# The latent keys' norm factor through DRAM, and the first heads' queries ahead of the first keys, in a two-layer decoder trunk

## The chip, the core and the metric

The kernel runs on one core of a Trainium2 chip. Five engines work side by side, each through its own instructions in order: PE (TensorE, matrix products into the PSUM memory), DVE (VectorE), ACT (ScalarE), POOL (GpSimd) and SP (SyncE, which here issues nearly all DMA transfers). They wait for one another by semaphores. The metric is the device time of one execution in microseconds (us). Before the change it is 1119.46 us, the median of three runs (1118.91 to 1119.87).

## The reference

The input is x of 512 tokens by 1024 features in float32. Two layers follow, each a token mixer and a squared-ReLU MLP (1024 to 4096 to 1024) with norms ahead and residuals. The first layer's mixer is a "forgetting" attention of 16 heads. The second is a multi-head latent attention of 8 heads, whose keys and values come from one compressed stream. The part that the change touches is the projection ahead of that second attention:

```python
src = rms_norm(stream, kv_norm_g)
kv_a = src @ w_kv_a                                   # 256 latent + 64 rotary columns
c_kv = rms_norm(kv_a[..., :KV_LORA_RANK], kv_a_norm_g)
k_rope = apply_rope(kv_a[..., KV_LORA_RANK:], cos, sin)
kv_b = (c_kv @ w_kv_b)                                # k_nope (128 a head) and v (128 a head)
c_q = rms_norm(h @ w_q_a, q_a_norm_g)                 # 384 latent columns
q = c_q @ w_q_b                                       # 128 without and 64 with rotation, a head
s = q_nope . k_nope + q_rope . k_rope                 # then scale, causal softmax, times v
```

A norm's factor 1/sqrt(mean of squares + eps) is one number per token. For `c_kv` it must be applied to tiles that have the features along the 128 partitions and the 512 tokens along the free axis, so each partition needs the whole row of 512 factors.

## The kernel before

**Arithmetic.** PE multiplies in a rounded float32 (fp32r). Each operand is split into a high part (a cast on ACT) and a low part (a subtraction on DVE), and a product is three matmuls: high by high, high by low, low by high (`three`, lines 272 to 281). `split` (204) makes the two parts of an activation tile: one ACT instruction, then one DVE instruction that waits for it. Almost everything is a 128 x 512 tile.

**Weights.** All weights lie in DRAM in the order in which they are used, cut into pieces (`pieces`, 75; the host's `_pack`, 1455, lays them out alike). Two raw buffers receive them by DMA from SP (`fetch`, 217), ACT casts the high part (`cast_piece`, 222) and DVE subtracts the low part (`low_piece`, 235). In the stage of the change this is done by hand with `prepare(n)` (1179): cast piece n, make its low part, and fetch piece n + 2 into the raw buffer that this frees. KA is the first of six pieces "ka" (the two compressing products). Behind them, KA+6 is "qb_r" (the rotary queries' weights of the first two heads, 384 columns), KA+7 "kvb_n" (the keys' weights of four heads, 1024), KA+8 "qb_n" (the first two heads' other queries, 768), KA+9 "kvb_v" (values, 1024).

**The stage.** From line 1177 to 1310 the order of the instructions on PE, DVE and ACT is as written (`order["on"]` chains each engine's instructions); SP's and POOL's is not, a planner places those. The planner also places everything behind line 1310 (the attention), and may put it ahead of the written chain's later instructions on the same engine. The stage computes `kv[0]`, `kv[1]` (latent keys), `krp` (rotary key) and `ql[0..2]` (latent queries) in PSUM, each in two halves (`low_rank`). Two factors along the tokens are made in it:

- The stream's norm factor (1203 to 1212): `token_sums` on PE puts the sums of squares of 128 tokens into each of four columns, `rsqrt_of(alone=True)` makes 1/sqrt on DVE with eleven tiny instructions, and then two DMAs turn the result: a write of 2 KB to DRAM (`line`) and a read of that row to all partitions (`row`, tile tag `rstd`). The row comes back with token p + 128 b at place 4 p + b, and is read with a stride of four elements (1227).
- The latent keys' norm factor (1252 to 1266): sums and 1/sqrt as before, and then `along_tokens(rs_kv)` (345): on PE, four products with the identity, two instructions each, put the row into a PSUM bank (`krow`, bank tag `tp`), and ACT copies it to SBUF (`kr`).

With `kr`, DVE scales both latent tiles by gain and factor (`ts`, 1270), ACT casts their high parts, DVE makes the low ones (`ckv`). Between these stand the third latent query (`low_rank(ql[2])`, `high(2)`, `low(2)`), the split of the rotary key (`krh`, `krl`), a square and two additions for the queries' factor. Then PE's order is: rotary queries `qb_r` (9 matmuls), keys of heads 0 to 3 from `ckv` (6 matmuls each, 1289), the queries' token sums, queries of heads 0 and 1 (9 matmuls each, 1302), and four blocks of values (`v_gen(0)`, 6 each). Three PSUM banks "acc" go round among these; a product waits until the tile three before it on "acc" has been split. `shift` and `rotate` turn the rotary queries, `stacked(a)` splits them, and POOL does most of the queries' 1/sqrt (`rs_q`). Then the attention begins, with further projections as filler between its steps.

Of the kernel before, what the change touches and what calls it, by code (L numbers as in the profile page):

```python
# [74 lines left out]
def pieces():  # L75

    out = [("f", 128)]
    out += [("qk", 1024)] * 2 + [("v", 1024)] * 4
    for p in range(1, FH // 2):
        out += [("v4", 1024)] * (2 * V4_BEFORE.count(p)) + [("qk", 1024)] * 2  # L80
    out += [("fo", 1024)] * 8
    out += [("ffn0", 1024)] * 40
    out += [("ka", 1024)] * 6
    q = [("qb_r", 384), ("qb_n", 768)]
    out += [q[0], ("kvb_n", 1024), q[1], ("kvb_v", 1024)] + q + [("kvb_n", 1024)] + q + q + [("kvb_v", 1024)]
    out += [("mo", 1024)] * 8
    out += [("ffn1", 1024)] * 32
    return out
# [11 lines left out]
def trunk(ctx: ExitStack, tc: tile.TileContext, xT, wts, gains, fing, rope, out):  # L100
# [63 lines left out]
    def nm(s):  # L164
        uid[0] += 1
        return f"{s}{uid[0]}"
# [7 lines left out]
    def tt(shape=(P, S)):  # L174
        return tp_.tile(list(shape), F32, tag="t", name=nm("t"))

    def f32(ap):
        return ap.bitcast(F32)
# [147 lines left out]
    def rsqrt_of(v, mult=1.0, alone=False, tags=("rs1", "rs2")):  # L326
        y, a = (small.tile([P, v.shape[-1]], F32, tag=t, name=nm("rs"), bufs=2 if t[:2] == "rs" else 1) for t in tags)

        nc.vector.tensor_single_scalar(a.bitcast(I32), v.bitcast(I32), 1, op=ALU.arith_shift_right)
        nc.vector.tensor_scalar(y.bitcast(I32), a.bitcast(I32), -1, RSQRT_BITS, op0=ALU.mult, op1=ALU.add)  # L330
        for step in range(3):
            m = mult if step == 2 else 1.0
            if alone:
                nc.vector.tensor_tensor(a, y, y, op=ALU.mult)
                nc.vector.scalar_tensor_tensor(out=a, in0=a, scalar=-0.5 * m, in1=v, op0=ALU.mult, op1=ALU.mult)
                nc.vector.scalar_tensor_tensor(out=y, in0=a, scalar=1.5 * m, in1=y, op0=ALU.add, op1=ALU.mult)
            else:

                nc.gpsimd.tensor_tensor(a, y, y, op=ALU.mult)
                nc.gpsimd.tensor_tensor(a, a, v, op=ALU.mult)  # L340
                nc.gpsimd.tensor_scalar(a, a, -0.5 * m, 1.5 * m, op0=ALU.mult, op1=ALU.add)
                nc.gpsimd.tensor_tensor(y, a, y, op=ALU.mult)
        return y
# [716 lines left out]
    def rt2():  # L1060
        return rp2.tile([P, S], F32R, tag="r2", name=nm("r2"))

    ctxs = []
    with ExitStack() as mx:
# [139 lines left out]

        em = small.tile([P, NB], F32, tag="em", name=nm("em"), bufs=1)
        nc.vector.tensor_scalar(em, vx, EPS, 0.0, op0=ALU.mult, op1=ALU.add)
        rs = rsqrt_of(vx, alone=True)
        line = keep.tile([S], F32, name=nm("line"))

        nc.sync.dma_start(line.rearrange("(p b) -> p b", b=NB), rs)  # L1210
        row = small.tile([P, S], F32, tag="rstd", name=nm("rstd"), bufs=2)
        nc.sync.dma_start(row, line.partition_broadcast(P))
        prepare(KA + 3)
        low_rank(kv[1], w[1][:4], hk, 0)
        low_rank(ql[0], w[1][4:], hm, 0)
# [7 lines left out]
        w = [blocks(piece("ka")) for _ in range(3)]  # L1223
        rotary_low(w[0][:4], 1)
        u, o = tt(), tt()
        ub, kb = (t.rearrange("p (b q) -> p b q", b=NB) for t in (u, krp))
        nc.vector.tensor_tensor(ub, kb, row.rearrange("p (q b) -> p b q", b=NB), op=ALU.mult)
        low_rank(kv[0], w[0][4:], hk, 1)
        for e in range(2):
            nc.scalar.copy(o[e * ROPE : (e + 1) * ROPE], u[(1 - e) * ROPE : (2 - e) * ROPE])  # L1230
# [22 lines left out]
        q_acc = tt()  # L1253
        square(q_acc, ql[0])
        high(0)
        rs_kv = rsqrt_of(mean(ss, KVR, em), alone=True)
        prepare(KA + 7)
        low(0)
        low_rank(ql[1], w[2][:4], hm, 1)
        krow = along_tokens(rs_kv)  # L1260
        sqs.append(tt())
        square(sqs[0], ql[1])
        high(1)
        low(1)
        kr = tt()
        nc.scalar.copy(kr, krow)
        ts = [tt(), tt()]
        ckv = [(rt2(), rt2()) for _ in range(2)]
        for b in range(2):
            nc.vector.scalar_tensor_tensor(out=ts[b], in0=kv[b], scalar=g("kva", b), in1=kr, op0=ALU.mult, op1=ALU.mult)  # L1270
            nc.scalar.copy(ckv[b][0], ts[b])
        low_rank(ql[2], w[2][4:], hm, 1)
        high(2)
        nc.vector.tensor_tensor(ckv[0][1], ts[0], f32(ckv[0][0]), op=ALU.subtract)
        low(2)
        nc.vector.tensor_tensor(ckv[1][1], ts[1], f32(ckv[1][0]), op=ALU.subtract)
        krh, krl = split(a)
        sqs.append(tt())
        square(sqs[1], ql[2])
# [4 lines left out]

        qp = bank("sc")
        linear(qp, piece("qb_r"), cq, nk=3)
        wk = piece("kvb_n")
        a, o = tt(), tt()
        for hd in range(4):
            kp_ = bank("acc" if hd < 3 else "tp")  # L1290
            linear(kp_, wk, ckv, nk=2, at=hd * 2 * P)
# [6 lines left out]

        rs_q = rsqrt_of(mean(ss, QR, em), -float((NOPE + ROPE) ** -0.5), tags=("rq1", "rq2"))
        prepare(KA + 10)  # L1300
        qw = piece("qb_n")
        for e in range(2):
            qp = bank("acc")
            linear(qp, qw, cq, nk=3, at=e * 3 * P)
            if e == 0:
                qr[0] = stacked(a)
            qn[e] = split(qp)
        for _ in v_gen(0):
            pass
        order["on"] = ()  # L1310
# [144 lines left out]
def _pack(i):  # L1455
# [38 lines left out]
    for p in range(4):  # L1494
        qs.append(_blk(qb[:, 2 * p : 2 * p + 2, NOPE:].reshape(QR, 2 * ROPE), slice(None)))
        qs.append(np.concatenate([_blk(qb[:, 2 * p + e, :NOPE], slice(None)) for e in range(2)], axis=1))
    parts += [qs[0], ns[0], qs[1], vs[0]] + qs[2:4] + [ns[1]] + qs[4:] + [vs[1]]
    parts += [_cols(i["mla_w_out"][0], f * P, P) for f in range(8)]
    parts += up(1)
    assert [x.size // P for x in parts] == [w for _, w in PIECES]  # L1500
# [48 lines left out]
```

## Time and profile before

| | |
|---|---|
| median of three runs | 1119.46 us |
| the profiled execution: time / span | 1119.58 us / 1117.5 us |
| PE busy | 1101.2 us, 99% of the span |
| DVE, ACT busy | 781.8 us (70%), 584.0 us (52%) |
| granted PE clock | 0.998 of full speed |
| the written stage | 594 to 648 us of the span |
| the second attention | 648 to about 752 us |

The span runs from the first to the last instruction; the time has some 2.1 us more around it. In rows of the timeline, the columns are start in us, duration in us, engine, line, operation, output <- inputs, shapes, count, and in brackets the idle time of the engine before it with what ended it. Rows show line 114 for almost all instructions, because a helper there records them; tiles tell them apart. Matmuls overlap: a row's duration is the modelled time through the array (0.39 us), while their starts lie closer together. So time that PE lost is read from starts.

### The profile page before, as it was taken

Reading aid. Unit: us, or ns where it says so; the run is one execution under the profiler, and the core shown is the slowest. Engines: PE = TensorE matmul, PEld = TensorE weight load, DVE = VectorE, ACT = ScalarE, POOL = GpSimd, SP = SyncE. Lnnn points to the kernel's source line nnn. Section 1 sums busy time; section 2 is a strip of 40 time slices with the busy share of each in tenths; the row PEclk is TensorE's granted clock in tenths of the full one; section 3 lists DMA queues with packets and bytes.
Section 4 is the critical chain, followed back from the end, with each engine's and each line's share of the span. In section 5 each row is a group of like instructions: output and inputs, shape, how many; then the busy total and the mean of one; then the engine's idle time right before and its main releaser. Section 6 shows DMA issues by size and latency. Waiting matters only on the chain.

```text
span 1117.5 us, 14137 instructions
## 1 busy us (share of the span) xinstructions
PE 1101.2 (99%) x5292; PEld 911.3 (82%) x5292; DVE 781.8 (70%) x1414; ACT 584.0 (52%) x1071; POOL 13.6 (1%) x46
## 2 busy tenths in 40 slices
PE   8999999999999999999999999999999999999997
PEld 6877887888888888888888888888888888888885
DVE  6899788864566667577896889736365775765784
ACT  5566565654555454434444768624675445444622
POOL 1000000001000000000000000000000000000000
PEclk9999999999999999999999999999999999999999
DMA  5322222142724315321345212214531611611401
GB/s 191 133 93 79 77 76 94 58 151 95 276 101 143 120 38 166 101 70 29 126 132 152 73 60 76 97 55 132 174 147 57 190 55 57 207 57 38 132 1 75
DMA packets 37108, 116.90 MB, mean 105 GB/s; under 512 B 4384, under 2 KB 5024, under 8 KB 37040
## 3 DMA queue, kind: packets, MB, share of 16 engines
q1 hardware_dynamic: 36176, 114.41, 31.2%
q10 hardware_dynamic: 864, 1.60, 0.4%
q8 instruction: 41, 0.67, 0.2%
q14 instruction: 27, 0.22, 0.1%
HBM read 109.67 MB, written 6.33 MB: 104 GB/s over the span
## 4 chain that ended last, share of the span: by engine, by line
PE 93%; DVE 4%; ACT 2%; DMA 0%; issue 0%; SPq 0%; ACTq 0%
PE up L114 35%; PE go L114 19%; PE acc L114 18%; PE tp L114 8%; PE keep L114 6%; PE sc L114 6%; DVE r L114 1%; DVE t L114 1%; ACT t L114 1%; ACT r L114 1%; DMA t<-xT 0%; DVE wlo L114 0%; DVE ptl L114 0%; DVE rs L114 0%; ACT whi L114 0%
## 5 line engine op out<-in xcount | busy, mean ns | idle before, releaser
L114 PE MATMUL up<-r,r 128*128 128x512 f32 x808 | 192.6, 390 | 0.0
L114 PE MATMUL acc<-r,whi 128*128 128x512 f32 x574 | 185.7, 404 | 5.0 <-ACT whi L114 5.0
L114 PEld LDWEIGHTS up<-r,r 128*128 128x128 f32 x808 | 151.3, 188 | 31.7
L114 PE MATMUL up<-r,whi 128*128 128x512 f32 x544 | 170.7, 390 | 0.0
L114 DVE TENSOR_TENSOR wlo<-raw,whi 128x1024 fp32r<-128x1024 f32 (+3 forms) x95 | 111.3, 1171 | 46.3 <-ACT whi L114 46.3
L114 DVE TENSOR_TENSOR t<-s,t 128x512 fp32r<-128x512 f32 x84 | 57.8, 688 | 118.4 <-ACT t L114 118.3
L114 ACT CAST whi<-raw 128x1024 fp32r<-128x1024 f32 (+3 forms) x95 | 95.5, 1008 | 80.1 <-PE acc L114 36.7
L114 ACT ACTIVATE s<-up 128x512 f32<-128x512 f32 x56 | 33.4, 597 | 184.6 <-PE up L114 184.6
L114 PEld LDWEIGHTS acc<-r,whi 128*128 128x128 f32 x574 | 105.9, 191 | 28.6 <-ACT whi L114 5.0
L114 PEld LDWEIGHTS up<-r,whi 128*128 128x128 f32 x544 | 101.8, 188 | 20.9
L114 PE MATMUL acc<-r,wlo 128*128 128x512 f32 x287 | 113.2, 395 | 0.0
L114 PE MATMUL up<-r,wlo 128*128 128x512 f32 x288 | 112.1, 389 | 0.0
L114 PE MATMUL go<-r,t 128*128 128x512 f32 x360 | 86.5, 389 | 0.0
L114 PEld LDWEIGHTS go<-r,t 128*128 128x128 f32 x360 | 67.6, 188 | 14.0
L114 PE MATMUL go<-whi,t 128*128 128x512 f32 x240 | 78.7, 389 | 0.0
L114 PE MATMUL sc<-r,r 128*128 128x512 f32 (+6 forms) x448 | 73.1, 346 | 1.7 <-ACT r L114 0.9
L114 PEld LDWEIGHTS sc<-r,r 128*128 128x128 f32 (+1 forms) x448 | 56.0, 187 | 16.7 <-issue 3.5
L114 PEld LDWEIGHTS acc<-r,wlo 128*128 128x128 f32 x287 | 54.6, 190 | 11.8 <-issue 0.4
L114 DVE TENSOR_TENSOR r<-raw,r 128x512 fp32r<-128x512 f32 x72 | 47.3, 696 | 23.6 <-ACT r L114 23.6
L114 PEld LDWEIGHTS up<-r,wlo 128*128 128x128 f32 x288 | 54.0, 188 | 11.2
L114 ACT ACTIVATE s<-s 128x512 f32<-128x512 f32 x64 | 40.5, 632 | 39.6 <-DVE s L114 37.8
L114 DVE TENSOR_TENSOR wlo<-q,whi 128x1024 fp32r<-128x1024 f32 x45 | 54.9, 1220 | 7.9 <-ACT whi L114 7.5
(202 smaller groups left out, 1879.7 us busy)
## 6 DMA issues: line engine op xcount, KB each, us to landing
raw<-wts SPq DMA_DIRECT2D x122, 512.0 KB, 3.5
q<-wts SPq DMA_DIRECT2D x56, 512.0 KB, 4.6
nb<-csc SPq DMA_DIRECT2D x8, 512.0 KB, 4.6
t<-xT SPq DMA_DIRECT2D x8, 256.0 KB, 6.2
r<-xT SPq DMA_DIRECT2D x8, 256.0 KB, 5.3
xmid<-r SPq DMA_DIRECT2D x8, 256.0 KB, 7.3
r<-xmid SPq DMA_DIRECT2D x8, 256.0 KB, 4.4
xkeep<-r SPq DMA_DIRECT2D x8, 256.0 KB, 2.1
```

Source lines behind the costliest of these rows:

```text
L114: ins = fn(*args, **kw)
```

## The change

Three things are changed, all between lines 1204 and 1308 and in the order of the weight pieces.

1. The two DMAs by DRAM become a helper, `by_dram`, used for both factors. The latent keys' factor loses `along_tokens` and the ACT copy; DVE's two scaling instructions read the row with a stride of four elements.
2. These two instructions, the two casts and the two subtractions of `ckv` move to behind the rotary queries' product in the written order, which is behind the additions for the queries' factor on DVE and behind the cast of piece KA+8 on ACT.
3. The first two heads' queries move ahead of the first four heads' keys on PE. The pieces are reordered to suit: KA+7 is now "qb_n" (768 columns), KA+8 "kvb_n" (1024). `stacked(a)` moves to ahead of the values, behind `prepare(KA + 10)`.

```diff
-    out += [q[0], ("kvb_n", 1024), q[1], ("kvb_v", 1024)] + q + [("kvb_n", 1024)] + q + q + [("kvb_v", 1024)]
+    out += q + [("kvb_n", 1024), ("kvb_v", 1024)] + q + [("kvb_n", 1024)] + q + q + [("kvb_v", 1024)]
...
-        rs = rsqrt_of(vx, alone=True)
-        line = keep.tile([S], F32, name=nm("line"))
-        nc.sync.dma_start(line.rearrange("(p b) -> p b", b=NB), rs)
-        row = small.tile([P, S], F32, tag="rstd", name=nm("rstd"), bufs=2)
-        nc.sync.dma_start(row, line.partition_broadcast(P))
+        def by_dram(r):
+            line = keep.tile([S], F32, name=nm("line"))
+            nc.sync.dma_start(line.rearrange("(p b) -> p b", b=NB), r)
+            row = small.tile([P, S], F32, tag="rstd", name=nm("rstd"), bufs=2)
+            nc.sync.dma_start(row, line.partition_broadcast(P))
+            return row.rearrange("p (q b) -> p b q", b=NB)
+        def by_block(t):
+            return t.rearrange("p (b q) -> p b q", b=NB)
+        row = by_dram(rsqrt_of(vx, alone=True))
...
-        rs_kv = rsqrt_of(mean(ss, KVR, em), alone=True)
+        kr = by_dram(rsqrt_of(mean(ss, KVR, em), alone=True))
         prepare(KA + 7)
         low(0)
         low_rank(ql[1], w[2][:4], hm, 1)
-        krow = along_tokens(rs_kv)
         sqs.append(tt())
         square(sqs[0], ql[1])
         high(1)
         low(1)
-        kr = tt()
-        nc.scalar.copy(kr, krow)
-        ts = [tt(), tt()]
-        ckv = [(rt2(), rt2()) for _ in range(2)]
-        for b in range(2):
-            nc.vector.scalar_tensor_tensor(out=ts[b], in0=kv[b], scalar=g("kva", b), in1=kr, op0=ALU.mult, op1=ALU.mult)
-            nc.scalar.copy(ckv[b][0], ts[b])
         low_rank(ql[2], w[2][4:], hm, 1)
         high(2)
-        nc.vector.tensor_tensor(ckv[0][1], ts[0], f32(ckv[0][0]), op=ALU.subtract)
         low(2)
-        nc.vector.tensor_tensor(ckv[1][1], ts[1], f32(ckv[1][0]), op=ALU.subtract)
         krh, krl = split(a)
         sqs.append(tt())
         square(sqs[1], ql[2])
         prepare(KA + 8)
         for t in sqs:
             add(q_acc, q_acc, t)
         qp = bank("sc")
         linear(qp, piece("qb_r"), cq, nk=3)
+        ts = [tt(), tt()]
+        ckv = [(rt2(), rt2()) for _ in range(2)]
+        for b in range(2):
+            nc.vector.scalar_tensor_tensor(
+                out=by_block(ts[b]), in0=by_block(kv[b]), scalar=g("kva", b), in1=kr, op0=ALU.mult, op1=ALU.mult
+            )
+            nc.scalar.copy(ckv[b][0], ts[b])
+        for b in range(2):
+            nc.vector.tensor_tensor(ckv[b][1], ts[b], f32(ckv[b][0]), op=ALU.subtract)
+        a, o = tt(), tt()
+        qw = piece("qb_n")
+        for e in range(2):
+            pp = bank("acc")
+            linear(pp, qw, cq, nk=3, at=e * 3 * P)
+            qn[e] = split(pp)
         wk = piece("kvb_n")
-        a, o = tt(), tt()
         for hd in range(4):
...
         prepare(KA + 10)
-        qw = piece("qb_n")
-        for e in range(2):
-            qp = bank("acc")
-            linear(qp, qw, cq, nk=3, at=e * 3 * P)
-            if e == 0:
-                qr[0] = stacked(a)
-            qn[e] = split(qp)
+        qr[0] = stacked(a)
         for _ in v_gen(0):
             pass
```

More of the change, by code (lines that the diff above doesn't have):

```diff
@@ L1225, in trunk @@
         u, o = tt(), tt()
-        ub, kb = (t.rearrange("p (b q) -> p b q", b=NB) for t in (u, krp))
-        nc.vector.tensor_tensor(ub, kb, row.rearrange("p (q b) -> p b q", b=NB), op=ALU.mult)
+        nc.vector.tensor_tensor(by_block(u), by_block(krp), row, op=ALU.mult)
         low_rank(kv[0], w[0][4:], hk, 1)
@@ L1496, in _pack @@
         qs.append(np.concatenate([_blk(qb[:, 2 * p + e, :NOPE], slice(None)) for e in range(2)], axis=1))
-    parts += [qs[0], ns[0], qs[1], vs[0]] + qs[2:4] + [ns[1]] + qs[4:] + [vs[1]]
+    parts += qs[:2] + [ns[0], vs[0]] + qs[2:4] + [ns[1]] + qs[4:] + [vs[1]]
     parts += [_cols(i["mla_w_out"][0], f * P, P) for f in range(8)]
```

## The prediction

> **What bounds the kernel now.** I read the page first: busy times and the chain of waits.
>
> ```profile
> PE 1101.2 (99%) x5292; PEld 911.3 (82%) x5292; DVE 781.8 (70%) x1414; ACT 584.0 (52%) x1071; POOL 13.6 (1%) x46
> ...
> PE 93%; DVE 4%; ACT 2%; DMA 0%; issue 0%; SPq 0%; ACTq 0%
> ```
>
> PE sets the time: 99% busy, and 93% of the chain that ended last. So an edit is worth what it takes from PE's work or from PE's waits. Next, the busy times in stretches around the change (columns: stretch, its length, then PE, PEld, DVE, ACT and POOL with counts, clock, DMA share, GB/s).
>
> ```profile
> 624.00:634.00 10.00, 9.84 (x48) 7.96 (x47) 9.20 (x14) 7.00 (x13) 0.00 (x0) 1.00 0.25 69
> ...
> 654.00:664.00 10.00, 9.46 (x58) 8.23 (x57) 9.13 (x28) 7.73 (x16) 0.00 (x0) 1.00 0.18 58
> ...
> 674.00:684.00 10.00, 8.90 (x60) 8.13 (x59) 8.44 (x26) 8.40 (x20) 0.00 (x0) 1.00 0.27 90
> ...
> 704.00:714.00 10.00, 10.00 (x54) 8.59 (x54) 8.21 (x20) 6.49 (x18) 0.00 (x0) 1.00 0.17 52
> ```
>
> PE is nearly full even in the stretch that is changed. The small gaps of 654 to 684 lie in the attention, where DVE is at 8.4 to 9.1 of 10. From 704 on PE is full and gives nothing back: what PE loses before stays lost. Third, PE's timeline where the factor is made and used:
>
> ```profile
> 624.42 1.05 PE L114 MATMUL tp<-ident,rs 128*128 128x128 f32 x8
> 625.23 0.71 PE L114 MATMUL acc<-r,whi 128*128 128x512 f32 x2
> ...
> 627.84 0.39 PE L114 MATMUL acc<-r,wlo 128*128 128x512 f32 x1
> 628.07 0.62 PE L114 MATMUL sc<-r,whi 128*128 128x512 f32 x2
> ...
> 629.97 0.50 PE L114 MATMUL sc<-r,whi 128*128 128x512 f32 x1 [0.16 <-DVE r L114]
> ...
> 630.55 0.62 PE L114 MATMUL acc<-r,whi 128*128 128x512 f32 x2
> ...
> 642.39 0.61 PE L114 MATMUL sc<-r,r 128*128 128x512 f32 x2
> 643.25 0.50 PE L114 MATMUL acc<-whi,r 128*128 128x512 f32 x1 [0.24 <-DVE r L114]
> ...
> 647.68 1.75 PE L114 MATMUL sc<-r,r 128*128 128x512 f32 x7
> ...
> 663.83 2.56 PE L114 MATMUL sc<-r,r 128*128 128x512 f32 x10 [0.54 <-DVE sm L114]
> ...
> 683.92 0.65 PE L114 MATMUL tp<-ident,t 128*128 128x128 f32 x4 [1.10 <-DVE r L114]
> ```
>
> The four products with the identity (tp<-ident,rs) hold PE from 624.42 to 625.23. `qb_r` takes 628.07 to 630.55 with a wait for DVE inside, and at 643.25 the second value block waits for a query's low part. A matmul of 512 columns costs 0.227, by twelve in a row in the chain of waits:
>
> ```profile
> 618.19 2.72 PE acc L114 x12
> ```
>
> **The change, part by part.**
>
> Removed from PE: the factor's spread, 625.23 - 624.42 = **-0.81**. Everything PE does behind it can come 0.81 earlier. The ACT copy behind it falls too, but ACT has gaps there. ACT's rows on the way that follows:
>
> ```profile
> 628.45 0.68 ACT L114 ACTIVATE r<-acc,gsb 128x512 fp32r<-128x512 f32 x1
> 629.03 0.61 ACT L114 CAST r<-t 128x512 fp32r<-128x512 f32 x1
> 629.95 0.60 ACT L114 ACTIVATE t<-acc 128x512 f32<-128x512 f32 x1 [0.31 <-DVE r L114]
> 630.45 0.82 ACT L114 CAST whi<-raw 128x768 fp32r<-128x768 f32 x1
> ...
> 633.48 0.59 ACT L114 CAST r<-acc 128x512 fp32r<-128x512 f32 x1 [0.17 <-PE acc L114]
> 633.96 1.05 ACT L114 CAST whi<-raw 128x1024 fp32r<-128x1024 f32 x1
> ...
> 636.85 0.59 ACT L114 CAST r<-tp 128x512 fp32r<-128x512 f32 x1
> ```
>
> Added, two DMAs. The same pair exists for the other factor:
>
> ```profile
> rstd<-line SPq DMA_DIRECT2D x1, 256.0 KB, 4.5
> ...
> line<-rs SPq DMA_DIRECT2D x1, 2.0 KB, 1.8
> ...
> 602.31 0.33 SPq L114 DMA_DIRECT2D line<-rs  x1
> 603.80 0.33 SPq L114 DMA_DIRECT2D raw<-wts  x1
> 604.18 0.42 SPq L114 DMA_DIRECT2D rstd<-line  x1
> ...
> 617.12 0.39 PE L114 MATMUL tp<-r,wlo 128*128 128x512 f32 x1
> ```
>
> The write lands 1.8 us behind its issue, and the read, 4.5 us behind its own with a fetch of 512 KB ahead of it. DVE finishes the new factor just before its next instruction, the low part of KA+7 at 623.99. DVE's rows:
>
> ```profile
> 612.92 1.05 DVE L114 TENSOR_TENSOR t<-sc,rstd 128x512 f32<-128x512 f32 x1
> ...
> 623.99 1.23 DVE L114 TENSOR_TENSOR wlo<-raw,whi 128x1024 fp32r<-128x1024 f32 x1
> ...
> 626.49 1.40 DVE L114 SCALAR_TENSOR_TENSOR t<-tp,gsb,t 128x512 f32<-128x512 f32 x2
> ...
> 629.17 0.75 DVE L114 SCALAR_TENSOR_TENSOR r<-acc,gsb,r 128x512 fp32r<-128x512 f32 x1 [0.55 <-ACT r L114]
> ...
> 632.18 1.41 DVE L114 TENSOR_TENSOR t<-t,t 128x512 f32<-128x512 f32 x2
> ...
> 642.50 0.69 DVE L114 TENSOR_TENSOR r<-acc,r 128x512 fp32r<-128x512 f32 x1
> ```
>
> So the row is there at about 624.0 + 1.8 + 4.5 = 630.4. The only things behind it on SP are fetches: KA+9 can go once KA+7's low part is made, KA+10 once KA+8's is (about 631.4, below); neither is cast before 638. SP itself then costs nothing.
>
> Moved: `ts` and `ckv`. In their new place DVE reaches them behind the additions for the queries' factor, and these wait on ACT. From the rows: `ql[2]`'s last matmul started at 627.84 and takes 0.39, now 0.81 sooner, so it ends at 627.4. ACT then runs high(2) at 627.5, the cast of krh at 628.1 (629.03 - 628.45 = 0.58 a step), the square at 628.7, and at 629.2 the cast of KA+8 (0.50 after the square, as 629.95 to 630.45). KA+8 is now the 1024-column piece: 1.05 us as in the row at 633.96, to 630.25. Its low part on DVE takes a step of 1.14 (623.99 to 625.13, the next start), to 631.4; the two additions 1.33 (632.18, 1.41 us for both less their overlap), to 632.75. Only now does DVE reach `ts`, 2.35 us after the row has landed. That is the cover of the DMAs.
>
> `ts` reads the row with a stride of four elements. No such three-operand instruction is in the trace. Bounds: 0.74 us each (both contiguous ones at 626.49, 1.40 with an overlap of some 0.07), and 1.05 by the strided two-operand row at 612.92, where the unstrided kin (632.18) take about 0.70. I take 1.05, since it is the same row's layout. [...]
>
> With 1.05, `ts` is at 632.75 and 633.8, done at 634.8. ACT's casts (0.62 each) end at 634.45 and 635.45, DVE's subtractions (0.69) at 635.45 and 636.15.
>
> PE meanwhile: `qb_r` starts at 628.07 - 0.81 = 627.26. It took 2.48 where nine matmuls at 0.227 take 2.04; low(2) is now ready at 627.5 + 0.68 + 0.75 = 628.9 and its reader wanted at 628.85, so I leave 0.2 of the 0.44: **-0.24**. Two queries, 18 matmuls, 4.08, fill PE until 633.6. They are the cover of the moved chain, and it isn't enough: the first key needs the first cast (634.5 with the hand-over), then the first subtraction (635.5), and its fifth matmul the second subtraction (636.2). It ends at 636.65; without a wait, 633.6 + 1.36 = 634.95. **+1.7**, which is 1.1 with 0.74 for `ts`. The next key takes the bank of the first query, whose low part stands on DVE behind those subtractions, 636.15 + 0.69 = 636.85: **+0.2**. Behind that PE has its keys without waits to 641.0, token sums (0.8), and values.
>
> `stacked(a)` moved. Before, it hid under the queries, though the value block at 643.25 waited for what came behind it on DVE: the two score matmuls at 642.39 need 0.45, so 643.25 - 642.84 = 0.4 was lost. That goes: **-0.4**. What is late next is the fourth value block, which takes the bank of the first. From the cast of the last key (636.85) to the end of the low part behind `stacked(a)` (642.50 + 0.69 = 643.19) it took 6.3; from the cast of the second key (633.48) to that of the last, 3.4. Now the second key ends at 638.2, the last key's cast comes at 641.6, and the first block's low part at about 647.7. PE has done three blocks at 641.8 + 4.1 = 645.9: **1.8 of possible wait**. The planner is free here to put the first scores ahead, as it did with two at 642.39; ten of 0.23 make 2.3, six of them need no rotated query. I take it as filled: 0, other end +1.8.
>
> POOL's part of the queries' factor:
>
> ```profile
> 640.64 0.44 POOL L339 TENSOR_TENSOR rs<-rs 128x4 f32<-128x4 f32 x1 [372.30 <-DVE rs L114]
> ...
> 645.59 0.20 POOL L342 TENSOR_TENSOR rs<-rs,rs 128x4 f32<-128x4 f32 x1
> ...
> 651.30 0.22 DVE L114 TENSOR_SCALAR sm<-sm,rs 128x2 f32<-128x2 f32 x1
> ```
>
> It spans 640.64 to 645.79, 5.15, and starts 3.8 behind the cast of the last key (636.85), since DVE makes the mean behind `rotate`. With that cast at 641.6 POOL runs from 645.4 to 650.5. Its result was first used at 651.30: the cover of 5.5 shrinks to 0.8, and I count nothing.
>
> Left: KA+7 and KA+8 swap sizes. KA+8's fetch, now the large one, goes out at 617.12 and is cast at 629.2, and KA+7's before it: both have landed. KA+7's own cast and low part get shorter, where ACT and DVE wait for the next product anyway. The sum: -0.81 - 0.24 + 1.7 + 0.2 - 0.4 = **+0.45 us**. Against the profiled 1119.58 (span 1117.5 and 2.08 around it) that is 1120.0; the median of the runs is 0.12 lower, so 1119.9. Rounded up for the part of the last block's wait that scores can't fill: **1120.0**. The attention's own waits, 0.54 and 1.10 (rows 663.83 and 683.92) besides smaller ones, are re-dealt by the planner: I take 0, ends -1.9 and +1.9.
>
> **The rivals.** A measurement of this kernel can tell some 0.2%, 2.24 us, from no change.
>
> *The last value block waits with nothing in its place* (slower). +0.45 + 1.8 = +2.25, 1121.7. It decides if fewer than some eight score matmuls stand ahead of that block on PE. For it: before, seven of ten scores stand behind the last block (647.68). Against: two did go into a wait. An attention that starts late meets a DVE at over 8 of 10 (654 to 684) that gives little back, so half of this case lies above 1121.7.
>
> *The keys don't wait.* If ACT and DVE get to `ts` sooner than reckoned, or the planner deals the attention better, what remains is -0.81 - 0.24 - 0.4 = -1.45, 1118.0; with the attention's two waits gone too, -3.1, 1116.4. For it: DVE stood idle for 0.55 ahead of 629.17, so it isn't full there. Against: DVE is in written order, and the cast of KA+8 stands before the additions.
>
> *The row comes late, or SP doesn't do it in the order written.* SP isn't chained: at 603.80 a fetch went between the write and the read. Should the planner put the fetch of KA+10 ahead of the read, the read goes at 631.5 and lands at 636.0, 3.25 behind DVE's need: 1123.2. If only the landing grows, it decides from 2.35 us on. [...]
>
> **How the numbers follow.** Forecast 0.48, last block's wait 0.25, keys without a wait 0.20, late row 0.07. Slower by over 0.2% is half or a little more of the second case, the fourth, and a tenth of the forecast: 0.25. Faster by over 0.2% (under 1117.2) is the part of the third with the attention's gain, and a little of the forecast: 0.10. Within: 0.65. The range reaches from 1117.4 (-2.1, the keys' gain with part of the attention's) to 1122.6 (+3.1, the unfilled wait with half of the attention's other end); the forecast's own is 1118.9 to 1121.2 (+0.45 with 0.6 less for `ts`, or with half of the last block's wait, and some 0.4 of the attention either way).
>
> **What would show it.** Right: PE's tp<-ident,rs is gone near 624; the two `ts` take 1.05 each and start near 632.7, right behind the additions, with the row landed by 631; PE waits near 634 to 636 for ACT and DVE ahead of the first key; ten scores, or most, lie ahead of the fourth value block near 646. Wrong: `ts` preceded by idle DVE (a late row), no wait ahead of the keys, the block waiting with PE empty, or a difference that lies mostly behind 650, in the attention.

## The result, and the profile after

The changed kernel takes **1121.19 us** (median of 19 runs, 1120.37 to 1122.41). The kernel before, timed beside it, takes 1119.19 us (19 runs, 1118.23 to 1120.13). The medians differ by 2.0 us, 0.18%; the ratio on record is 1.0020, with a 95% interval of 1.0013 to 1.0026. So the kernel is slower, by more than the interval leaves to chance, and the loss lies at the very edge of the 0.2% that the prediction called "within": the interval has both sides of it. The forecast was 1120.0, +0.54 over the 1119.46 that it started from.

The profiled execution took 1122.41 us (span 1120.4, mean PE clock 0.996). It is the slowest of the 19, for a reason shown below. Two lines of its page, the busy times and the engines' shares of the chain that ended last:

```profile
PE 1102.4 (98%) x5284; PEld 911.0 (81%) x5284; DVE 782.8 (70%) x1414; ACT 583.3 (52%) x1070; POOL 13.6 (1%) x46
...
PE 94%; DVE 3%; ACT 2%; DMA 1%; issue 0%; SPq 0%; ACTq 0%
```

PE has eight instructions fewer (x5292 before) and still sets the end. Its timeline where the waits were forecast:

```profile
633.12 0.39 PE L114 MATMUL acc<-r,wlo 128*128 128x512 f32 x1
634.50 0.50 PE L114 MATMUL acc<-r,whi 128*128 128x512 f32 x1 [0.99 <-ACT r L114]
635.49 0.50 PE L114 MATMUL acc<-r,whi 128*128 128x512 f32 x1 [0.49 <-DVE r L114]
...
636.87 1.22 PE L114 MATMUL acc<-r,whi 128*128 128x512 f32 x2
...
651.96 0.39 PE L114 MATMUL acc<-r,whi 128*128 128x512 f32 x1
```

PE ends the queries at 633.35 (633.12 + 0.23) and then waits twice: 0.99 for ACT's cast and 0.49 for DVE's subtraction, both of the first key. Those are the two waits that the prediction named. DVE's and SP's timelines on the way there, and then the two transfers (KB each, median us from issue to landing):

```profile
632.70 2.14 DVE L114 SCALAR_TENSOR_TENSOR t<-tp,gsb,rstd 128x512 f32<-128x512 f32 x2
...
623.91 0.33 SPq L114 DMA_DIRECT2D line<-rs  x1
...
626.99 0.33 SPq L114 DMA_DIRECT2D rstd<-line  x1
```

In the view of DMA issues:

```profile
rstd<-line SPq DMA_DIRECT2D x1, 256.0 KB, 4.1
line<-rs SPq DMA_DIRECT2D x1, 2.0 KB, 3.1
```

The row goes out at 623.91, the read at 626.99 (write landed in 3.1, not 1.8), and the row is there at 631.1, 1.6 us before the scalings ask for it at 632.70. No idle time stands ahead of them: the DRAM trip was hidden. The two scalings take 1.07 each, where the contiguous form takes 0.70 (1.40 for both in the kernel before): in this three-operand instruction too the operand with the stride of four elements costs extra, 0.37 each.

What the prediction did not have is in the row at 636.87: two matmuls that take 1.22 instead of 0.62. The stretches of one microsecond show why (third column from the end: granted PE clock):

```profile
636.00:637.00 1.00, 1.00 (x5) 0.45 (x4) 1.00 (x3) 0.46 (x1) 0.00 (x0) 0.92 0.00 0
637.00:638.00 1.00, 1.00 (x4) 0.81 (x4) 0.74 (x2) 0.92 (x2) 0.00 (x0) 0.50 0.00 0
...
640.00:641.00 1.00, 1.00 (x5) 0.84 (x4) 0.55 (x1) 1.00 (x2) 0.00 (x0) 0.87 0.00 0
```

The two stretches left out, to 640, read 0.50 too. So PE ran at half its clock for about 3.4 us (3 in full, and of the outer two twice what they lack, 0.16 and 0.26), right behind the two waits.

**Where the 2 us arise.** The starts of four groups split each execution: the latent keys' token sums (sc<-ones, near 620), the queries' token sums (the same group, near 640), the first product behind the values, and the last product of the second MLP (go, x48, from the chain of waits). PE's timeline and the chain in the kernel before (649.27 is the first matmul on "acc" behind the scores):

```profile
620.75 0.94 PE L114 MATMUL sc<-ones,t 128*128 128x1 f32 x8
...
636.00 0.95 PE L114 MATMUL sc<-ones,t 128*128 128x1 f32 x8
...
649.27 0.62 PE L114 MATMUL acc<-r,whi 128*128 128x512 f32 x2
```

In the chain of waits:

```profile
1098.19 11.22 PE go L114 x48
```

The same in the changed kernel:

```profile
620.56 0.95 PE L114 MATMUL sc<-ones,t 128*128 128x1 f32 x8
...
642.65 0.95 PE L114 MATMUL sc<-ones,t 128*128 128x1 f32 x8
```

In the chain of waits:

```profile
1100.94 11.22 PE go L114 x48
```

From the first to the second group: 15.25 before, 22.09 after (this holds the two queries, 4.1 us of work, only after). From the first group to the product behind the values (649.27 and 651.96): 28.52 and 31.40, so +2.88. From there to the last product: 448.92 and 448.98. So the attention and the MLP behind the stage give back or take less than 0.1, and nearly the whole difference lies in 30 us of the written stage. From the last product to the end of the span it is 19.31 and 19.46.

### The profile page after: what moved, and what is told of

Same layout as the page of the kernel before. It is cut to its first block, busy times and chain, and to the rows that moved or that the text cites. A ratio compares the mean times of both kernels' runs of the same rounds, so it can differ in the third digit from the quotient of the medians.

```text
span 1120.4 us, 14124 instructions
## 1 busy us (share of the span) xinstructions
PE 1102.4 (98%) x5284; PEld 911.0 (81%) x5284; DVE 782.8 (70%) x1414; ACT 583.3 (52%) x1070; POOL 13.6 (1%) x46
## 4 chain that ended last, share of the span: by engine, by line
PE 94%; DVE 3%; ACT 2%; DMA 1%; issue 0%; SPq 0%; ACTq 0%
PE up L114 35%; PE acc L114 19%; PE go L114 19%; PE tp L114 8%; PE keep L114 6%; PE sc L114 6%; DVE t L114 1%; DVE r L114 1%; ACT t L114 1%; DMA t<-xT 1%; ACT r L114 0%; DVE wlo L114 0%; DVE ptl L114 0%; ACT whi L114 0%; DVE fs L114 0%
```

## The experiments

Each was timed beside the kernel before; differences are between the medians of one comparison. "Stage" is the stretch just used, from the latent keys' token sums to the first product behind the values: 28.52 before.

### The changed kernel again: is the half clock always there?

No edit.

> The changed kernel once more, beside the next ones. Theory A (in every execution some 1.7 us of waits, and in those in which the granted clock falls to half after PE's wait, 1.2 us more): times spread from +1.4 to +3 over the kernel before, median +2.0; a profile with the clock at 1.00 throughout would have q1 start 30.2 us after the latent keys' token sums (that point in the profile at hand: 31.4 with a half-clock stretch), one with a half-clock stretch 31.4. Rival B: always the same, with a half-clock stretch in every execution.

1120.65 against 1118.67 us, +1.98, ratio 1.0018 (1.0009 to 1.0027). Its profiled execution is free of the half clock (1.00 in every stretch from 632 to 642), with the same waits. So theory A holds, and this execution can be split without the clock. Rows of its PE timeline, then the last product:

```profile
619.93 0.95 PE L114 MATMUL sc<-ones,t 128*128 128x1 f32 x8
...
628.63 0.62 PE L114 MATMUL acc<-r,whi 128*128 128x512 f32 x2
...
633.88 0.50 PE L114 MATMUL acc<-r,whi 128*128 128x512 f32 x1 [1.00 <-ACT r L114]
634.86 0.50 PE L114 MATMUL acc<-r,whi 128*128 128x512 f32 x1 [0.48 <-DVE r L114]
...
636.23 0.73 PE L114 MATMUL acc<-r,whi 128*128 128x512 f32 x2
...
640.45 0.95 PE L114 MATMUL sc<-ones,t 128*128 128x1 f32 x8
...
645.48 3.09 PE L114 MATMUL sc<-r,r 128*128 128x512 f32 x10
648.56 0.51 PE L114 MATMUL acc<-whi,r 128*128 128x512 f32 x1
...
650.06 0.62 PE L114 MATMUL acc<-r,whi 128*128 128x512 f32 x2
```

In the chain of waits:

```profile
1099.01 11.22 PE go L114 x48
```

| step (by starts on PE) | before | after | difference | forecast |
|---|---|---|---|---|
| token sums to `qb_r` (628.07; 626.33 after, 628.63 - 2.30) | 7.32 | 6.40 | -0.92 | -0.81 |
| `qb_r` (to 630.55; 628.63) | 2.48 | 2.30 | -0.18 | -0.24 |
| keys (to 636.00; from 632.72 to 640.45) | 5.45 | 7.73 | +2.28 | +1.9 |
| queries and token sums (to 641.03; 4.09 and 0.80) | 5.03 | 4.89 | -0.14 | 0 |
| values and scores (to 649.27; from 641.25 to 650.06) | 8.24 | 8.81 | +0.57 | -0.4 |
| stage | 28.52 | 30.13 | +1.61 | +0.45 |

From 650.06 to the last product it is 448.95 again, and from there to the end of the span 19.49, about 0.2 longer than before. Together +1.8, where the medians differ by 1.98 to 2.0. The half clock of the first profile adds 31.40 - 30.13 = 1.27. How many executions have it is open. A stretch of 3.4 us at half is 0.0015 of the mean clock. Over the 30 runs of this kernel the mean was 0.996 in five, whose times average 1121.8, and 0.997 or more in the other 25, which average 1121.0; none of the kernel before's 68 runs beside the experiments was at 0.996. But the mean does not single such executions out: the profile of the longer wait below has a half-clock stretch at a mean of 0.997. Five of 30 is a rough guess, and only two executions were profiled, one with the stretch and one without.

The last step of the table is set by DVE and ACT. Their timelines in the same profile:

```profile
643.83 0.84 ACT L114 CAST whi<-raw 128x768 fp32r<-128x768 f32 x1 [0.81 <-DMA raw<-wts]
...
644.92 1.43 DVE L114 TENSOR_TENSOR wlo<-raw,whi 128x384 fp32r<-128x384 f32 x2
646.38 1.41 DVE L114 TENSOR_TENSOR r<-t,r 64x512 fp32r<-64x512 f32 x2
```

All ten scores stand ahead of the fourth value block, as taken (645.48, x10), but the block starts at 648.56, 3.08 behind them; ten scores need 2.27, so 0.81 is lost. The wait was forecast at 1.8. The two pieces in one row at 644.92 are KA+10 and KA+11. KA+11 is no part of the written stage, the planner places it. In the kernel before, on DVE's timeline, its low part stood behind `stacked(a)`'s two subtractions:

```profile
641.06 1.40 DVE L114 TENSOR_TENSOR r<-t,r 64x512 fp32r<-64x512 f32 x2
...
643.11 0.95 DVE L114 TENSOR_TENSOR wlo<-raw,whi 128x768 fp32r<-128x768 f32 x1
```

Now its cast (643.83) and its low part come ahead. The low part takes a step of 0.87 on DVE (1.46 for both pieces, 0.59 for KA+10 alone before), and `stacked(a)`, and behind it, at 647.82, the low part that the fourth block needs, come so much later. The cast's own wait of 0.81 for its fetch costs nothing here: DVE has no idle time from 641.91 on to 649.62.

### PE kept busy in its wait

```diff
+        busy = bank("tp")
+        for n in range(8):
+            mm(busy, qw[0][:, :P], cq[0][0], start=n == 0, stop=n == 7)
         wk = piece("kvb_n")
```

The eight matmuls are added work; nothing reads their result.

> The changed kernel with eight more matmuls (8 x 0.227 = 1.8 us) on PE between the second query and the first key, where PE waited 633.35 to 635.5. Their result, in a spare bank, is used by nothing; all else is as in the changed kernel. Theory A (the half clock at 636.9 to 640.4 comes from PE's idle time just before it): with the idle time filled, the granted clock stays at 1.00 in every 1-us stretch of 634 to 642, the keys run at 0.227 a matmul, and the time falls by up to 1.7 us against the changed kernel, to +0.3 to +1.3 us over the kernel before. Rival B (the half clock has another cause, or the records only mismark it): a half-clock stretch appears again, and the time stays at +2.0. If PE's queue were delayed by the added work itself, the time would rise to about +3.

1120.74 against 1118.87, +1.87, ratio 1.0016 (1.0007 to 1.0024). PE is full and the clock whole. PE's timeline, then one of the stretches, all of which read 1.00 from 632 to 642:

```profile
633.07 1.98 PE L114 MATMUL tp<-r,whi 128*128 128x512 f32 x8
...
636.60 0.74 PE L114 MATMUL acc<-r,whi 128*128 128x512 f32 x2
```

In the stretches of one microsecond:

```profile
637.00:638.00 1.00, 1.00 (x6) 0.81 (x5) 0.77 (x2) 0.91 (x2) 0.00 (x0) 1.00 0.00 0
```

The second key starts 16.32 behind the token sums (620.28), in the changed kernel 16.30. So the waits cost what they cost whether PE idles or not; the loss that all executions share isn't the clock. Theory A had the clock right and the time wrong: it gave +0.3 to +1.3, and the time stayed at the rival's +2. In none of these 11 runs is the mean clock below 0.997, and none is above 1121.19. That fits a half clock that needs the idle time, but since the changed kernel too has executions without it, one whole profile and eleven mean clocks are no proof.

### A longer wait

```diff
+        spare = tt()
+        for t in (sqs[0], sqs[1]):
+            add(spare, q_acc, t)
         ts = [tt(), tt()]
```

Two additions whose result nothing reads, on DVE ahead of the scalings.

> The changed kernel with two more additions on DVE ahead of the scalings (1.3 us, results unused), so that PE's wait ahead of the first key is 1.3 us longer (about 3.4 in place of 2.1). Theory A (half clock follows from PE's idle time): a half-clock stretch near 637 in the profile, and the time +1.3 for the wait and up to 1.2 for the clock above the changed kernel's fast executions: +3.0 to +4.5 over the kernel before. Rival B: +2.9 to +3.3, with the clock at 1.00.

1123.75 against 1118.67, +5.08, ratio 1.0042 (1.0028 to 1.0056). PE's timeline, then the first and the last of the four stretches with a lower clock:

```profile
635.83 0.50 PE L114 MATMUL acc<-r,whi 128*128 128x512 f32 x1 [2.44 <-ACT r L114]
636.82 0.80 PE L114 MATMUL acc<-r,whi 128*128 128x512 f32 x1 [0.48 <-DVE r L114]
```

In the stretches of one microsecond:

```profile
636.00:637.00 1.00, 0.52 (x2) 0.20 (x3) 0.92 (x3) 0.81 (x2) 0.00 (x0) 0.70 0.00 0
...
639.00:640.00 1.00, 1.00 (x4) 0.77 (x4) 0.03 (x1) 0.62 (x2) 0.00 (x0) 0.60 0.00 0
```

The wait is 2.44 + 0.48 instead of 1.00 + 0.48. The scalings start 13.59 behind the token sums (620.44) instead of 12.14, so the two additions cost 1.45, and the first key 15.39 instead of 13.95, 1.44 later: DVE's chain sets the first key one for one. The stage is 32.72: 30.13, plus 1.44, plus 1.15 that is left for a half clock of 3.4 us again (0.30, two full stretches of 0.50, and 0.40 short, times two), close to the 1.27 above. The median of +5.08 lies above both recorded ranges. The profiled execution's parts give +4.4 (4.20 in the stage, 0.2 at the end of the span); the rest is not explained, though two of the five executions have a mean clock of 0.994, below the profiled one's 0.997.

### Keys ahead of queries, as before, with the DRAM trip

```diff
-    out += q + [("kvb_n", 1024), ("kvb_v", 1024)] + q + [("kvb_n", 1024)] + q + q + [("kvb_v", 1024)]
+    out += [q[0], ("kvb_n", 1024), q[1], ("kvb_v", 1024)] + q + [("kvb_n", 1024)] + q + q + [("kvb_v", 1024)]
...
-        qw = piece("qb_n")
-        for e in range(2):
-            pp = bank("acc")
-            linear(pp, qw, cq, nk=3, at=e * 3 * P)
-            qn[e] = split(pp)
         wk = piece("kvb_n")
...
-        qr[0] = stacked(a)
+        qw = piece("qb_n")
+        for e in range(2):
+            qp = bank("acc")
+            linear(qp, qw, cq, nk=3, at=e * 3 * P)
+            if e == 0:
+                qr[0] = stacked(a)
+            qn[e] = split(qp)
```

The host's `_pack` is reordered alike, and `stacked(a)` is back at its old place.

> The changed kernel with the keys ahead of the queries again, pieces in their old order, the rotated queries' split at its old place; factor through DRAM and late scalings as in the changed kernel. Theory A (the queries ahead are the cover of the DMAs and of DVE's queue): PE reaches the first key near 629.3 and waits for the casts until 634.5 and the second subtraction until 636.2, some 5.5 us in place of 1.9; the clock falls to half behind it; +4 to +6.5 over the kernel before. Rival E (the moved split is the main cost): less than the changed kernel's +2.

1125.44 against 1118.8, +6.64, ratio 1.0059 (1.0043 to 1.0075). PE's timeline, then the first of the seven stretches with a lower clock:

```profile
632.99 0.79 PE L114 MATMUL acc<-r,whi 128*128 128x512 f32 x1 [4.61 <-ACT r L114]
```

In the stretches of one microsecond:

```profile
632.00:633.00 1.00, 0.01 (x1) 0.01 (x1) 1.00 (x2) 0.62 (x1) 0.00 (x0) 0.52 0.00 0
```

With nothing between `qb_r` and the keys PE waits 4.61, and the clock is half from 632 to nearly 639 (0.57 in the last stretch), 6.8 us, two times 3.4. The queries are the cover, as theory A has it (with +6.64 a little above its +6.5), and the order is worth 4.7 us to the new route (6.64 - 1.98), the price of the longer half clock included.

### The scalings ahead of the additions

The block with `ts`, the casts and the subtractions stands above `for t in sqs: add(...)`; nothing else differs.

```diff
+        ts = [tt(), tt()]
...
+            nc.vector.tensor_tensor(ckv[b][1], ts[b], f32(ckv[b][0]), op=ALU.subtract)
         for t in sqs:
             add(q_acc, q_acc, t)
         qp = bank("sc")
         linear(qp, piece("qb_r"), cq, nk=3)
-        ts = [tt(), tt()]
...
-            nc.vector.tensor_tensor(ckv[b][1], ts[b], f32(ckv[b][0]), op=ALU.subtract)
```

> The changed kernel with the two scalings, casts and subtractions of the latent keys moved ahead of the two additions on DVE (1.33 us earlier there). Theory A (PE's wait ahead of the first key is what costs): the row lands near 631.3, DVE starts the scalings at 631.4, the first key's wait falls from 2.1 us to about 0.7, the clock doesn't drop, and the time is -0.5 to +0.5 us against the kernel before (1.3 to 2.5 below the changed kernel). Rival C (the wait is only passed on, to the value blocks behind or the attention): time within 0.5 us of the changed kernel, +1.5 to +2.5.

1120.66 against 1118.87, +1.79, ratio 1.0018 (1.0009 to 1.0027): nothing won. The timelines of PE and DVE:

```profile
633.33 0.50 PE L114 MATMUL acc<-r,whi 128*128 128x512 f32 x1 [0.43 <-DVE r L114]
...
636.03 0.73 PE L114 MATMUL acc<-r,whi 128*128 128x512 f32 x2 [1.20 <-DVE r L114]
...
630.52 2.15 DVE L114 SCALAR_TENSOR_TENSOR t<-tp,gsb,rstd 128x512 f32<-128x512 f32 x2
...
633.97 1.41 DVE L114 TENSOR_TENSOR t<-t,t 128x512 f32<-128x512 f32 x2
```

The scalings start at 630.52, right behind the low part of KA+8, and PE waits only 0.43 in the first key. But the additions now stand on DVE at 633.97, ahead of the queries' low parts (from 635.29), and the second key, which takes the first query's bank, waits 1.20. Rival C holds, with the second key in place of its value blocks: the wait was passed on, since DVE has the same list to work off before that key, which starts 16.32 behind the token sums (619.71), in the changed kernel 16.30. It also shows that the row is there by 630.5.

### PE's way for the factor, all else as changed

`by_dram` for the latent keys goes back to `along_tokens` and the ACT copy, and the scalings read that contiguous copy.

```diff
-        kr = by_dram(rsqrt_of(mean(ss, KVR, em), alone=True))
+        rs_kv = rsqrt_of(mean(ss, KVR, em), alone=True)
...
+        krow = along_tokens(rs_kv)
...
+        kr = tt()
+        nc.scalar.copy(kr, krow)
...
-                out=by_block(ts[b]), in0=by_block(kv[b]), scalar=g("kva", b), in1=kr, op0=ALU.mult, op1=ALU.mult
+                out=by_block(ts[b]), in0=by_block(kv[b]), scalar=g("kva", b), in1=by_block(kr), op0=ALU.mult, op1=ALU.mult
```

> The changed kernel with the latent keys' factor made by the products with the identity and the ACT copy, as before the change, at their old places; the scalings stay late and the queries ahead. PE has 0.81 us more, the scalings read a contiguous copy laid out by blocks (0.74 instead of 1.07 us each). Theory A: the first key starts 0.6 us sooner relative to DVE and PE arrives 0.81 later, so its wait falls from 2.1 to about 0.7; clock stays up; time +0.0 to +1.0 over the kernel before. Rival D (DVE's place for the scalings is all that matters, whoever makes the factor): +1.5 to +2.5, with the same wait.

1120.53 against 1118.87, +1.66, ratio 1.0015 (1.0006 to 1.0023). PE's timeline at the first key:

```profile
634.81 0.50 PE L114 MATMUL acc<-r,whi 128*128 128x512 f32 x1 [0.63 <-ACT r L114]
635.54 0.50 PE L114 MATMUL acc<-r,whi 128*128 128x512 f32 x1 [0.22 <-DVE r L114]
```

The stage is 30.32 against 30.13: of the 0.92 that the DRAM trip takes off PE, only 0.2 is left. PE comes to the first key later here and waits 0.63 + 0.22 instead of 1.00 + 0.48, and the contiguous scalings take 0.70 each (1.40 for both) instead of 1.07. So the time is rival D's, while the shorter wait is theory A's: the gain on PE ends at the same DVE chain. The 0.2 is below what the times can tell; the medians lie 0.3 the other way.

### The order alone

As the last, and `ts` and `ckv` back in their old places as well. What remains of the change is the queries ahead of the keys and `stacked(a)` ahead of the values.

```diff
         nc.scalar.copy(kr, krow)
+        ts = [tt(), tt()]
...
+            nc.scalar.copy(ckv[b][0], ts[b])
         low_rank(ql[2], w[2][4:], hm, 1)
         high(2)
+        nc.vector.tensor_tensor(ckv[0][1], ts[0], f32(ckv[0][0]), op=ALU.subtract)
         low(2)
+        nc.vector.tensor_tensor(ckv[1][1], ts[1], f32(ckv[1][0]), op=ALU.subtract)
```

> Only the third part of the change: queries ahead of keys, pieces reordered, the split of the rotated queries ahead of the values; factor and scalings as before the change. Theory A (the order itself costs nothing): no wait ahead of the keys, -0.5 to +0.5 us against the kernel before. Rival E (the moved split makes the fourth value block wait and delays the attention): +1 to +2 us, with PE's wait at the fourth value block and not at the first key.

1119.49 against 1118.87, +0.62, ratio 1.0003 (0.9994 to 1.0012): not to be told from no change by the times. In the trace PE has no wait at the keys; the stage is 29.02, +0.50, and there is one loss, ahead of the fourth value block (PE's and DVE's timelines):

```profile
645.00 3.11 PE L114 MATMUL sc<-r,r 128*128 128x512 f32 x10
...
644.45 1.43 DVE L114 TENSOR_TENSOR wlo<-raw,whi 128x384 fp32r<-128x384 f32 x2
```

Ten scores fill 2.27 of a wait of 3.1 (the next block starts at 648.10), with KA+10 and KA+11 ahead of `stacked(a)` on DVE: the same 0.8 as in the changed kernel. So it belongs to the new order, not to the DRAM trip. Which part of the order is not shown: no run moves the queries without `stacked(a)`. Rival E had the place, at a higher price.

### The row in the order of the tokens

The stride is taken away by writing the row in token order, so that the scalings read it contiguously.

```diff
-        kr = by_dram(rsqrt_of(mean(ss, KVR, em), alone=True))
+        rs_kv = rsqrt_of(mean(ss, KVR, em), alone=True)
+        line2 = keep.tile([S], F32, name=nm("line"))
+        nc.sync.dma_start(line2.rearrange("(b p) -> p b", p=P), rs_kv)
+        kr = small.tile([P, S], F32, tag="rstd", name=nm("rstd"), bufs=2)
+        nc.sync.dma_start(kr, line2.partition_broadcast(P))
...
-                out=by_block(ts[b]), in0=by_block(kv[b]), scalar=g("kva", b), in1=kr, op0=ALU.mult, op1=ALU.mult
+                out=ts[b], in0=kv[b], scalar=g("kva", b), in1=kr, op0=ALU.mult, op1=ALU.mult
```

> The changed kernel with the latent keys' factor written to DRAM in the tokens' own order (512 single elements in place of 128 groups of four), so that the row comes back contiguous and the scalings read it without a stride. Theory A: the scalings take 0.74 in place of 1.07 us each, the first key's wait falls by 0.65, and the distance from the token sums to q1 is 29.5 us instead of 30.2, time +1.0 over the kernel before, if the write lands no later than 3.5 us behind its issue. Rival F (the scattered write is slow): the row lands after 632.7 and DVE is idle ahead of the scalings; each us late is a us lost, +2 or more.

1128.74 against 1118.67, +10.07, ratio 1.0087 (1.0073 to 1.0101). The timelines of SP and PE:

```profile
623.72 0.38 SPq L114 DMA_DIRECT2D line<-rs  x1
...
635.51 0.33 SPq L114 DMA_DIRECT2D rstd<-line  x1
...
640.71 1.52 PE L114 MATMUL acc<-r,whi 128*128 128x512 f32 x2 [7.39 <-ACT r L114]
```

512 writes of one element take 11.8 us to land (623.72 to 635.51), where 128 writes of four took 3.1. DVE waits 6.66 for the row, PE 7.39, and the clock is half for 6.8 us. The scalings do take 0.70 each. Rival F holds: the strided write costs far more than the strided read saves.

### The stage in another order

`shift` goes ahead of the scalings, and these ahead of the additions; the additions and `rotate` go between the keys, and KA+9 one key sooner; `stacked(a)` is cut in two halves around the first value block (`half(e)` is the cast and the subtraction of one query).

```diff
-        for t in sqs:
-            add(q_acc, q_acc, t)
...
+        shift(o, qp, range(4))
         ts = [tt(), tt()]
...
-            if hd == 1:
+            if hd == 0:
+                for t in sqs:
+                    add(q_acc, q_acc, t)
                 prepare(KA + 9)
-            shift(o, qp, range(hd, hd + 1))
-        rotate(a, o, qp)
+            if hd == 2:
+                rotate(a, o, qp)
...
-        qr[0] = stacked(a)
-        for _ in v_gen(0):
+        half(0)
+        next(values0)
+        half(1)
+        for _ in values0:
```

> The changed kernel with the order of the stage worked out anew: the four shifts of the rotary queries on ACT right behind the cast of KA+8 (ACT was idle for 3.6 us there), the scalings ahead of the additions on DVE, the additions behind the first key's split, the rotation behind the third, the two halves of the rotated queries' split around the first value block. Theory A (the 1.7 us are nothing but waits on DVE's order): waits of 0.5 at the first key, 0.3 at the second, the fourth value block's wait filled by scores; q1 27.8 to 28.3 us behind the token sums (28.5 before), time -0.7 to 0.0 against the kernel before. Rival G (DVE's work in the stage is the bound, 25 of 29 us busy before, and 0.65 more with the stride): no better than +0.5.

1118.49 against 1118.67, -0.18, ratio 0.9998 (0.9990 to 1.0007). The changed kernel's loss is gone, as theory A has it (-0.7 to 0.0), where rival G had +0.5 or more, and there is no gain. PE's timeline, from the first key to the queries' token sums:

```profile
632.67 0.42 PE L114 MATMUL acc<-r,whi 128*128 128x512 f32 x1
633.51 0.50 PE L114 MATMUL acc<-r,whi 128*128 128x512 f32 x1 [0.43 <-DVE r L114]
...
639.11 0.95 PE L114 MATMUL sc<-ones,t 128*128 128x1 f32 x8
```

PE's one wait at the keys is 0.43. From the token sums to the end of the span it takes 496.72 us (before 496.75, the changed kernel again 498.57). The scores interleave differently here, so the stage cannot be cut at the same place, but the trace shows where the gain on PE went. PE comes to the first key 12.79 behind the token sums (619.88), as in the changed kernel. That is 1.1 sooner than before, counted with the queries (9.80 to the keys, and 4.09 for two queries). The keys then hold it for 6.44, where 24 matmuls take 5.45, so 1.0 of the 1.1 is lost again in them: most of it at the row with the wait, the rest in rows just behind it that start late. From the queries' token sums to the last product it takes 458.00, against 457.97 before without the queries (462.19 less 4.22), and the end of the span is 0.2 longer.

The same order with PE's way for the factor (the edit of "PE's way", on this kernel):

> The reordered stage of the earlier experiment, but with the latent keys' factor from the products with the identity and the ACT copy, as before the change (PE +0.81, DVE -0.65 by unstrided scalings). Theory G (in the reordered stage DVE, idle for hardly 3 us between 629.5 and 648, is the bound, so that the DRAM route's gain on PE is eaten by its stride on DVE): -0.4 to +0.4 us against the reordered stage with DRAM, so about -0.6 to +0.4 against the kernel before. Theory A alone (PE's work and waits decide, and the reordered waits stay small): +0.8 against the reordered stage with DRAM.

1119.36 against 1118.8, +0.56, ratio 1.0007 (0.9997 to 1.0016). The DRAM trip is ahead by 0.34 in the trace (497.06 against 496.72 from the token sums to the end) and by 0.74 in the differences of medians. A's 0.8 fits the medians and G's at most 0.4 the trace, so the totals don't tell them apart. In the trace the trip brings PE to the keys 0.92 sooner (12.79 against 13.71), the keys take back 0.38 (6.44 against 6.06), and the end of the span 0.15, so part of what PE gains goes to DVE's list, as in G. The trip's worth in a good order lies somewhere from 0.3 to 0.7 us, and neither kernel beats the one before.

## Why the prediction was right, and where its sum was not

The time fell inside the range, and the direction and the keys' wait were right. How near the number came is in part luck: the range was 5.2 us wide, 1121.19 lies within 0.01 of the end of the forecast's own (1121.2), and as a difference the 2.0 us are nearer to the first rival's 2.25 than to the forecast. The sum was 1.2 us short: +0.45, where the stage lost 1.61. Step by step, with times from the token sums of the latent keys (620.75 in the forecast's rows, 619.93 in the second profile):

- *The factor's spread and `qb_r`, -0.81 and -0.24.* Measured -0.92 and -0.18, together -1.10 for -1.05. Right.
- *The DRAM trip is covered.* Right, though not by its own figures: the write landed in 3.1 instead of 1.8, the read in 4.1 instead of 4.5. The forecast gave 2.35 us of cover, the trace 1.6. SP did write, fetch, read, in that order, so the late row did not come.
- *The first key waits for DVE's and ACT's chain, +1.7 and +0.2.* The mechanism is right to its two waits and their releasers. The scalings were forecast at 12.00 and came at 12.14, the first key's work on PE at 12.85 and 12.79, the second key at 16.10 and 16.30. With three keys at 4.22 instead of 4.09 that makes +2.28 for +1.9: a term 0.4 too small, made of small steps.
- *`stacked(a)` moved, -0.4, and the last value block's wait of 1.8 "taken as filled".* This is **the term that was mis-sized**. The fill was right: all ten scores went ahead, where the forecast had only bounded it by two of before. The wait wasn't: the block was forecast ready at 26.95 and was at 28.63, while PE came to it at 25.55 instead of 25.15, so 1.8 became 3.1 and ten scores left 0.81. Of the 1.68 that the block was late, 0.2 is a slip in the sum (the last key's cast at 641.6 and the interval of 6.3 make 647.9, not 647.7), 0.5 is the keys' lateness (that cast came at 21.36, forecast 20.85), and 0.87 is KA+11's low part. The interval of 6.3 was carried over from a trace in which that low part stood behind `stacked(a)` (643.11); in the new order it stood ahead. No run moves that low part alone; this split is read from the traces. The row stood in the trace of before; the forecast did not ask on which side of the moved instruction it would come. So the first rival (the block waits unfilled) came true for less than half of its price, by a longer wait and not by fewer scores.
- *POOL's factor and the attention, 0.* The stretch behind the stage is 448.95 us, 448.92 before. Right, and much closer than the ends of 1.9 either way: in none of the kernels in which it can be cut at that place does it differ from before by more than 0.1.
- *Not in the forecast at all*: the half clock behind the wait, +1.27 in one of the two profiled executions, and about 0.2 us at the end of the span. The second rival (the keys don't wait, 1118.0) fell, and the nearest kernel to it, with the stage in another order, showed 1118.49 and no gain.

## What to carry to other kernels

A moved chain pays off on the engine that is freed only as far as the next engine's list allows: here PE was freed of 0.9 us and DVE's list set the first key just the same, so count what DVE and ACT still have to do before the consumer, not what PE no longer does. When an interval is carried over from the old trace to a moved instruction, go through every instruction inside and just behind it, those that a planner places too, and ask on which side each will come. And look at the granted clock behind a new wait on PE: here waits of 0.99 + 0.49 us had 3.4 us of half clock behind them in one of two profiles.

## What was not expected of the hardware

- **PE's clock was at half around some waits.** It was at half for 3.4 us behind waits of 0.99 + 0.49 us (in one of two profiles) and of 2.44 + 0.48, and for 6.8 us with waits of 4.61 and of 7.39. One stretch of 3.4 us cost 1.15 to 1.27 us of the stage, less than the 1.7 of clock, in part since a later wait shrank: the fourth value block's from 0.81 to 0.54 in the first profile (2.81 from 647.68 to 650.48, less 2.27 of scores). Why it comes in one execution and not in another is not shown: the changed kernel's second profile, with waits of 1.00 + 0.48, has the clock at 1.00 in every stretch from 632 to 642. That PE's idle time is the cause is argued from where the stretches stand, not proven; behind the shortest waits with a half clock PE was idle for only some 1.5 to 1.9 us and had matmuls on either side.
- **The same small write to DRAM took very different times.** 128 pieces of 16 bytes landed in 1.8 us (the stream's factor before) and 3.1 us (here); 512 pieces of four bytes, in 11.8.
- **The end of the span** is some 0.2 us longer behind the last product in all seven kernels with a second DRAM trip (19.46 to 19.54) than in the four without it (19.28 to 19.34). The issue of the last output transfer comes 15.5 behind that product in both kernels (1113.70 and 1116.44), so the difference lies behind it, 3.8 against 4.0. No run here shows the cause.
